# A hybrid gMLP / gated delta rule layer in three phases, with most of its large products formed by Strassen's method

## The chip, the cores and the metric

The kernel runs on one core of a Trainium2 chip. The metric is device time in microseconds of one execution. Engines are named as in the profile: PE (TensorE, the matrix engine), PEld (its weight loads), DVE (VectorE), ACT (ScalarE), POOL (GpSimd) and SP (SyncE, which here only issues DMAs). A matmul takes a stationary block (the weight load) and streams the columns of a moving block past it; "columns" below are those of the moving block.

## The reference

One layer takes 2048 prompt tokens and 8 single sample tokens through one combined projection, two branches and a merge. Cut to its core:

```python
h = rmsnorm(x, pre_g)
u_a, v_a, z_a, qkv, z_b, a_b, b_b, gate_a, gate_b = jnp.split(h @ w_in, splits, axis=-1)
y_a = u_a * (W_s @ rmsnorm(v_a) + b_s) * silu(z_a)          # 128-position chunks, tril W_s
q, k, v = silu(short_conv(qkv, width 4));  q, k = l2norm(q), l2norm(k)
# gated delta rule per head: S_t = a_t S_{t-1} + k_t beta_t (v_t - a_t S_{t-1}^T k_t)^T,  o_t = S_t^T q_t
y_b = rmsnorm(o, gdn_g) * silu(z_b)
merged = sigmoid(gate_a) * (y_a @ w_pa) + sigmoid(gate_b) * (y_b @ w_pb)
out = x + rmsnorm(merged @ w_out, post_g)
```

The model width is 1024, with 8 heads of 128. There are 12 kinds of large products, each 2056 tokens by 1024 by 1024: nine column groups of `w_in` (u, v, z, q, k, v of the conv, z_b, gate a, gate b), and `w_pa`, `w_pb`, `w_out`. All is fp32. The outputs are also the new conv rows, the matrix states and the normalised v rows.

## The kernel before

**Tiling.** The tokens are cut in two halves: f = 0 with 1024 tokens and f = 1 with 1024 tokens and the 8 samples. `TBS` cuts half 0 in 2 blocks of 512 columns and half 1 in 3 of 344. Every fp32 factor is held as the sum of a high and a low part in the type fp32r, and a product takes three matmuls for each of 8 blocks of 128 features: high by high, high by low, low by high.

**The stream of products.** A `Job` is one block of 128 output features. `load()` brings its 512 KB of weights, `split()` makes the parts (ACT the high one at L147, DVE the low one in two pieces at L149), `products()` puts 24 matmuls per token block on PE at L161, and the job's `evac` takes the result out of PSUM. `run()` goes through all jobs of half 0, of half 1 and of the end phase, loading and splitting one job ahead.

**What lies between the products.** `products()` counts streamed columns, and after every `STRIDE` = 2800 it calls `step()`, which advances one generator of each of four queues: chains (`chq`), small work (`smq`), convolutions (`cvq`) and heads (`bgq`). The order of instructions on every engine follows from these calls. `head()` does one head of one half: transposes of k and q, KD, E, M and AT, then a substitution of 31 dependent steps on DVE (L511 to L513: shuffle, multiply, subtract), spread over 28 yields, then the merge of its blocks to X and Y. `chain()` then goes through 8 chunks of 128 tokens, one after another: p (PE), r (DVE, L585), pz (PE), w (ACT, L591), pu (PE), S (DVE, L596), and S is what the next p needs. O is the output of a chunk.

**Where.** The sixteen heads (8 of each half) lie beside the products of `w_in`; the products of `w_pa`, `w_pb` and `w_out` come last, from about 2160 us, with no head beside them. The normalised x is built by `build_h()` (L245 and its split L203/L204). The beginning has its own order for the v products of half 0 (L933).

Of the kernel before, what the change touches and what calls it, by code (L numbers as in the profile page):

```python
# [25 lines left out]
PIN = True  # L26


def hybrid_step(tc, d):
    nc = tc.nc  # L30
    if PIN:
        mm = lambda *a, **k: tc.keep_in_program_order(nc.tensor.matmul(*a, **k))  # L32
        transpose = lambda *a, **k: tc.keep_in_program_order(nc.tensor.transpose(*a, **k))  # L33
    else:
        mm, transpose = nc.tensor.matmul, nc.tensor.transpose
    top = ExitStack()
    cp = top.enter_context(tc.tile_pool(name="cp", bufs=1))
    ap = top.enter_context(tc.tile_pool(name="apool", bufs=1))
    wp = top.enter_context(tc.tile_pool(name="wp", bufs=2))
    tp = top.enter_context(tc.tile_pool(name="tp", bufs=3))  # L40
    dp = top.enter_context(tc.tile_pool(name="dp", bufs=1, space=DRAM))
    pa = top.enter_context(tc.tile_pool(name="pa", bufs=3, space=PSUM))

    dma = nc.sync.dma_start

    def big():
        return tp.tile([P, 3, 344], F32, tag="big", name="big", bufs=4)

    flat = lambda t: t.rearrange("p a b -> p (a b)")

# [19 lines left out]
    S = cp.tile([P, NH, P], F32, name="S")  # L70
    nc.gpsimd.memset(S, 0.0)
# [3 lines left out]
    ssx = cp.tile([P, 17], F32, name="ssx")  # L75
    nc.gpsimd.memset(ssx[:, 16:17], 1.0)
# [3 lines left out]
    nwt = cp.tile([P, 64], F32, name="nwt")  # L80

# [1 line left out]
    m_sp = [[dp.tile([P, WT[f]], F32, name=f"m{f}_{g}") for g in range(8)] for f in range(2)]  # L83
    ya_sp = [dp.tile([8, P, WT[f]], F32, name=f"ya{f}") for f in range(2)]
# [39 lines left out]
    class Job:  # L124
        def __init__(self, w, acts, tbs, evac, pre=None, mid=None, m=P):
            self.w, self.acts, self.tbs, self.evac, self.pre, self.mid, self.m = w, acts, tbs, evac, pre, mid, m
            self.raw = self.hi = self.lo = self.ahead = None

        def last(self, b):
            return b == len(self.tbs) - 1  # L130

    def load(j):
        if j.raw is None:
            j.raw = wp.tile([P, KB, P], F32, tag="raw", name="raw", bufs=1)
            dma(j.raw[:, :, :j.m], j.w)

    def load_apart(j):
        j.raw = sp.tile([P, KB, P], F32, tag="KD", name="raw1", bufs=2)
        dma(j.raw, j.w)

    def split(j):
        if j.hi is None:
            load(j)
            j.hi = wp.tile([P, KB, P], F32R, tag="hi", name="hi")
            j.lo = wp.tile([P, KB, P], F32R, tag="lo", name="lo")
            m = j.m
            nc.scalar.activation(j.hi[:, :, :m], j.raw[:, :, :m], AF.Copy)  # L147
# [3 lines left out]
    streamed = [0]

    def products(j, b):
        off, w = j.tbs[b]
        ah, al = j.acts
        ps = pa.tile([P, 512], F32, tag="acc", name="acc")
        out = ps[:j.m, :w]
        i = 0
        for k in range(KB):
            for wt, at in ((j.hi, ah), (j.hi, al), (j.lo, ah)):  # L160
                nc.tensor.matmul(out, wt[:, k, :j.m], at[:, k, off:off + w], start=(i == 0), stop=(i == 23))  # L161
                i += 1
                streamed[0] += w
                if streamed[0] >= STRIDE:
                    streamed[0] -= STRIDE
                    step()
        j.evac(b, ps, off, w)
        if j.mid:
            j.mid(b)

    def run(groups):
        jobs = [j for g in groups for j in g]
        pos = 0
        for g in groups:
            for j in g:
                split(j)
                if j.pre:
                    j.pre()
            last = g[-1]
            nxt = jobs[pos + len(g): pos + len(g) + 2]  # L180
            for b in range(len(last.tbs)):
                if g[0].ahead:
                    g[0].ahead(b)
                for j in g:
                    if b == 0 and nxt:
                        load(nxt[0])
                    if len(g) == 1:
                        if b == 1 and nxt:
                            split(nxt[0])
                    elif j is last and j.last(b) and nxt:  # L190
                        split(nxt[0])
                    products(j, b)
            pos += len(g)

    def wblk(i):
        return d["w_blk"][i]

# [1 line left out]
    def new_set(pool, pre):  # L199
        return [pool.tile([P, KB, 1032], F32R, name=pre + n) for n in "hl"]  # L200
# [12 lines left out]
    def build_h(f, off, w, at, start=False):  # L213
# [27 lines left out]
        while got:  # L241
# [5 lines left out]
            if todo:  # L247
                got.append(fetch())
# [996 lines left out]
```

## Time and profile before

| | |
|---|---|
| runs | 2706.78 us median of 3 (2701.3 to 2707.1) |
| span of the profiled execution | 2705.5 us |
| PE matmul busy | 2615.8 us, 97% |
| PE weight load busy | 2334.3 us, 86% |
| DVE / ACT / POOL busy | 1553.0 / 1044.4 / 420.7 us |
| moved by DMA | 280 MB, 31% of the queues' time |
| chain that ended last | PE 78%, DVE 11%, DMA 5%, ACT 3% |

The profiled execution lies 1.3 us below the median of the runs. The busy time of a matmul is longer than the distance to the next one, since matmuls follow each other in a pipeline; so counts times start-to-start distances tell what PE needs, and busy time tells only where it stood still.

### The profile page before, as it was taken

The page shows a single profiled execution, that of the slowest core. Times are in us where ns is not written, and L with a number is a line of the kernel's source. Part 1 is how long each engine was busy: PE and PEld are TensorE (multiplying, and loading weights), DVE is VectorE, ACT ScalarE, POOL GpSimd, SP SyncE. Part 2 cuts the span into 40 slices and gives each one's busy share as a digit, 9 for nine tenths or more (in the row PEclk, how much of TensorE's full clock was granted, in tenths as well). Part 3 has the DMA queues.
Part 4 walks back from the last instruction along what each step waited for, and adds up shares of the span by engine and source line. Part 5 has one row for each costly group of instructions (what it writes and reads, how often), then busy time and mean ns, then how long its engine had stood idle before and what let it go on. Part 6 is the DMA issues. An engine that isn't in the chain of part 4 may idle for free.

```text
span 2705.5 us, 42484 instructions
## 1 busy us (share of the span) xinstructions
PE 2615.8 (97%) x15755; PEld 2334.3 (86%) x15755; DVE 1553.0 (57%) x5001; ACT 1044.4 (39%) x2728; POOL 420.7 (16%) x535
## 2 busy tenths in 40 slices
PE   7989999999999999989999999999998999999998
PEld 6778788887788888989999999999998988999886
DVE  6266866765765725356668657567565444442454
ACT  5323453453453423423534534534431332332121
POOL 2021111121121102022112211211202102102000
PEclk9989999999999999999999999999999999999999
DMA  6232212211211223123122122112145676645442
GB/s 205 79 121 63 67 43 71 86 44 59 79 44 67 86 77 115 48 70 108 56 65 68 48 76 72 42 68 75 46 133 202 221 245 233 243 168 183 136 141 95
DMA packets 139792, 280.38 MB, mean 104 GB/s; under 512 B 19944, under 2 KB 75688, under 8 KB 139584
## 3 DMA queue, kind: packets, MB, share of 16 engines
q1 hardware_dynamic: 139584, 277.66, 31.0%
q8 instruction: 124, 2.03, 0.3%
q14 instruction: 84, 0.69, 0.1%
HBM read 205.06 MB, written 72.55 MB: 103 GB/s over the span
## 4 chain that ended last, share of the span: by engine, by line
PE 78%; DVE 11%; DMA 5%; ACT 3%; issue 1%; POOL 1%; SPq 0%; DVEq 0%; ACTq 0%; POOLq 0%
PE acc L161 64%; PE p L32 2%; PE acc L933 2%; PE O L32 2%; DVE vT L653 2%; PE trn L33 2%; PE pu L32 1%; PE g L32 1%; DVE lo L149 1%; PE pz L32 1%; PE pk L32 1%; DMA m<-mo 1%; DVE bc L511 1%; DVE nwt L96 1%; DMA xt<-in_x_tok 1%
## 5 line engine op out<-in xcount | busy, mean ns | idle before, releaser
L161 PE MATMUL acc<-Ah,hi 128*128 128x344 f32 (+1 forms) x3360 | 1202.2, 358 | 1.4 <-ACT Ah L203 1.4
L161 PE MATMUL acc<-Ah,lo 128*128 128x344 f32 (+1 forms) x3360 | 1201.0, 357 | 0.3 <-DVE lo L149 0.3
L161 PE MATMUL acc<-Al,hi 128*128 128x344 f32 (+1 forms) x3360 | 1199.4, 357 | 0.5 <-DVE Al L204 0.2
L161 PEld LDWEIGHTS acc<-Al,hi 128*128 128x128 f32 x3360 | 636.1, 189 | 57.7 <-DVE Al L204 1.4
L161 PEld LDWEIGHTS acc<-Ah,lo 128*128 128x128 f32 x3360 | 636.6, 189 | 57.1 <-DVE lo L149 0.6
L161 PEld LDWEIGHTS acc<-Ah,hi 128*128 128x128 f32 x3360 | 636.2, 189 | 57.1 <-ACT Ah L203 1.9
L149 DVE TENSOR_TENSOR lo<-raw,hi 128x512 fp32r<-128x512 f32 x370 | 266.3, 739 | 313.4 <-ACT hi L147 278.8
L147 ACT ACTIVATE hi<-raw 128x1024 fp32r<-128x1024 f32 x185 | 195.3, 1056 | 320.6 <-PE acc L161 282.8
L513 DVE TENSOR_TENSOR Yc<-Yc,tmp 128x248 f32<-128x248 f32 (+30 forms) x496 | 148.6, 300 | 10.2
L511 DVE STREAM_SHUFFLE bc<-Uc 128x248 f32<-128x248 f32 (+30 forms) x496 | 151.1, 309 | 0.0
L512 DVE TENSOR_TENSOR tmp<-bc,Yc 128x248 f32<-128x248 f32 (+30 forms) x496 | 145.7, 294 | 0.5
L481 POOL TENSOR_TENSOR kl<-kq,kh 128x256 fp32r<-128x256 f32 x128 | 97.9, 773 | 238.1 <-ACT kh L480 237.9
L653 DVE SCALAR_TENSOR_TENSOR kq<-craw,convw,kq 128x1024 f32<-128x1024 f32 x96 | 122.6, 1277 | 1.1
L591 ACT ACTIVATE w<-pz,s_bb 128x128 f32<-128x128 f32 x128 | 46.9, 367 | 184.4 <-PE pz L32 184.1
L585 DVE SCALAR_TENSOR_TENSOR r<-p,neg,NV 128x128 f32<-128x128 f32 x128 | 44.2, 346 | 126.7 <-PE p L32 126.2
L161 PE MATMUL acc<-Bh,hi 128*128 128x344 f32 (+1 forms) x320 | 111.9, 350 | 0.0
L161 PE MATMUL acc<-Bh,lo 128*128 128x344 f32 (+1 forms) x320 | 111.9, 350 | 0.0
L161 PE MATMUL acc<-Bl,hi 128*128 128x344 f32 (+1 forms) x320 | 111.6, 349 | 0.0
L1101 POOL TENSOR_TENSOR g<-g,u 128x344 f32<-128x344 f32 (+1 forms) x40 | 45.1, 1128 | 349.1 <-DVE g L1100 344.9
L637 ACT ACTIVATE craw<-acc 128x344 f32<-128x344 f32 (+1 forms) x120 | 61.1, 509 | 94.1 <-PE acc L161 93.8
L446 ACT ACTIVATE junk<-trn 128x128 f32<-128x128 f32 x256 | 67.4, 283 | 42.3 <-PE trn L33 42.3
L1100 DVE TENSOR_TENSOR g<-g,acc 128x344 f32<-128x344 f32 (+1 forms) x40 | 23.2, 581 | 101.6 <-PE acc L161 83.5
(321 smaller groups left out, 3485.3 us busy)
## 6 DMA issues: line engine op xcount, KB each, us to landing
raw<-in_w_blk SPq DMA_DIRECT2D x136, 512.0 KB, 3.7
g<-big SPq DMA_DIRECT2D x16, 516.0 KB, 3.2
g<-g SPq DMA_DIRECT2D x16, 516.0 KB, 4.8
xt<-in_x_tok SPq DMA_DIRECT2D x16, 512.0 KB, 4.8
m<-mo SPq DMA_DIRECT2D x32, 256.0 KB, 3.1
G<-gc SPq DMA_DIRECT2D x16, 512.0 KB, 9.0
g<-big SPq DMA_DIRECT2D x16, 512.0 KB, 2.8
yb<-yT SPq DMA_DIRECT2D x32, 256.0 KB, 2.3
```

Source lines behind the costliest of these rows:

```text
L32: mm = lambda *a, **k: tc.keep_in_program_order(nc.tensor.matmul(*a, **k))
L33: transpose = lambda *a, **k: tc.keep_in_program_order(nc.tensor.transpose(*a, **k))
L147: nc.scalar.activation(j.hi[:, :, :m], j.raw[:, :, :m], AF.Copy)
L149: nc.vector.tensor_tensor(j.lo[:, p, :m], j.raw[:, p, :m], j.hi[:, p, :m].bitcast(F32), ALU.subtract)
L161: nc.tensor.matmul(out, wt[:, k, :j.m], at[:, k, off:off + w], start=(i == 0), stop=(i == 23))
L446: nc.scalar.activation(junk, tr[:, tk(n)], AF.Square, accum_out=acc[:, c:c + 1])
L481: nc.gpsimd.tensor_tensor(kl, kq[:, :, tk(c)], kh.bitcast(F32), ALU.subtract)
L511: nc.vector.stream_shuffle(bc[:, :, l + 1:], Uc[:, :, l + 1:], [l] * 32)
L512: nc.vector.tensor_tensor(tmp[:, :, l + 1:], bc[:, :, l + 1:], Yc[:, :, l:l + 1].to_broadcast([P, 8, 31 - l]), ALU.mult)
L513: nc.vector.tensor_tensor(Yc[:, :, l + 1:], Yc[:, :, l + 1:], tmp[:, :, l + 1:], ALU.subtract)
L637: nc.scalar.activation(raw[:, 3 + off:3 + off + w], ps[:, :w], AF.Copy)
L653: nc.vector.scalar_tensor_tensor(acc, raw[:, i:i + HALF], convw[:, blk, i:i + 1], acc, ALU.mult, ALU.add)
```

## The change

The kernel is cut in three phases, and the tokens of half 1 in two quarters of 516 columns (512 prompt tokens and 4 samples each; `NQ`), each streamed as 2 × 258.

**Phase 1** forms v, the three conv kinds, z, u of both halves, and z_b of half 0. Two blocks of 128 output features are taken as a `Pair`, and with the two quarters of tokens they form a 2 × 2 by 2 × 2 block product: `seven()` takes 7 products of 4 feature blocks each where the plain way takes 8. `weights()` forms the 7 weight operands of a pair, split in parts; `refill()` forms the 7 token operands of a half once, at the start and at the switch to half 1. k, q, v, z_b, m and y_a of all heads go to DRAM. **Phase 2** forms z_b of half 1, both gates and `w_pa` by plain products (L754), and all sixteen heads lie beside these; `fetch_unit()` brings a head's k, q, v back. A `step()` now comes every 1700 columns, and the substitution has 12 yields. **Phase 3** forms `w_pb` and `w_out` by `seven()`.

```diff
-TB3 = [(0, 344), (344, 344), (688, 336)]
-TBS = [[(0, 512), (512, 512)], [(0, 344), (344, 344), (688, 344)]]
-STRIDE = 2800
+NQ = [512, 516]
+TBS = [[(0, 512), (512, 512)], [(0, 258), (258, 258), (516, 258), (774, 258)]]
+PACE = [2800, 1700, 2800]
...
+    def parted(src, tag, k):
+        hi, lo = wtile(tag + "h", k=k), wtile(tag + "l", k=k)
+        nc.scalar.activation(hi, src, AF.Copy)
+        nc.vector.tensor_tensor(lo, src, hi.bitcast(F32), ALU.subtract)
...
+    def weights(p):
+        r1, r2 = wtile("r1", F32), wtile("r2", F32)
+        dma(r1, p.w1)
+        dma(r2, p.w2)
+        yield
+        a, b, c, e = r1[:, 0:4, :], r1[:, 4:8, :], r2[:, 0:4, :], r2[:, 4:8, :]
+        p.wt[0], p.wt[2] = parted(r1, "wa", 8)
+        nc.gpsimd.tensor_tensor(a, a, c, sub)
+        nc.vector.tensor_tensor(c, c, e, add)
+        yield
+        p.wt[5] = parted(e, "wx", 4)[0]
+        nc.vector.tensor_tensor(e, e, a, sub)
+        nc.gpsimd.tensor_tensor(b, b, e, sub)
+        yield
+        p.wt[4], p.wt[1] = parted(r2, "wc", 8)
+        yield
+        p.wt[3], p.wt[6] = parted(r1, "wb", 8)
...
+        for k in range(4):
+            for wp_, at in ((hi, ah), (hi, al), (lo, ah)):
+                for b in range(n // w):
+                    nc.tensor.matmul(ps[:m, b, :w], wp_[:, k, :m], at[:, k, b * w:(b + 1) * w], ...)
+                    stream(w)
...
+    def seven(p, ops, n, nxt, after):
+        A = acc()
+        go(0, A)
+        nc.scalar.activation(cv(s1[:, :n], n), pv(A, n), AF.Copy)
+        B = acc()
+        go(1, B)
+        nc.vector.tensor_tensor(cv(u2[:, :n], n), pv(B, n), cv(s1[:, :n], n), ALU.add)
+        go(2, A)
+        p.evac(0, 0, A, None, n)
+        go(3, B)
+        nc.vector.tensor_tensor(cv(u3[:, :n], n), pv(B, n), cv(s1[:, :n], n), ALU.add)
+        C = acc()
+        go(4, C)
+        p.evac(1, 1, C, u3, n)
+        go(5, B)
+        p.evac(1, 0, B, s1, n)
+        go(6, C)
+        p.evac(0, 1, C, u2, n)
...
-            if (l + 1) * 28 // 31 > l * 28 // 31:
+            if (l + 1) * 12 // 31 > l * 12 // 31:
                 yield
```

With `n` = 516 a product is 24 matmuls of 258 columns, with `n` = 512 it is 12 of 512 columns. The numbers of pairs are 28 (half 0) and 24 (half 1) in phase 1, and 4 of each width plus 8 of 512 columns in phase 3.

How the order stands on the engines, at three places. First DVE, where the convolutions of k and q of the first head lie. Before (`lo` is a weight's low part, L650 and L653 the convolution, `mo` the gMLP mix, `rx` a statistic of x):

```order
L149 TENSOR_TENSOR lo<-raw,hi 128x512
L650 TENSOR_SCALAR kq<-craw,convw 128x1024
L418 SCALAR_TENSOR_TENSOR mo<-mx,vecs,bb 128x512
L98 SCALAR_TENSOR_TENSOR rx<-nwt,rx 128x9
L653 SCALAR_TENSOR_TENSOR kq<-craw,convw,kq 128x1024
L418 SCALAR_TENSOR_TENSOR mo<-mx,vecs,bb 128x512
L653 SCALAR_TENSOR_TENSOR kq<-craw,convw,kq 128x1024
L149 TENSOR_TENSOR lo<-raw,hi 128x512
L653 SCALAR_TENSOR_TENSOR kq<-craw,convw,kq 128x1024
```

After, on DVE in one pair of a conv kind in phase 1 (`wal`, `wxl`, `wcl`, `wbl` are low parts of weights, `r` their sums, `u` and `q<-acc` sums out of PSUM, L559 the convolution):

```order
L217 TENSOR_TENSOR u_3033<-acc,s_3015 128x512
L559 SCALAR_TENSOR_TENSOR q<-q,convw 128x512 x6
L146 TENSOR_TENSOR wal<-r_2987,wah 128x1024
L225 TENSOR_TENSOR u_3068<-acc,s_3015 128x512
L158 TENSOR_TENSOR r_2988<-r_2988 128x512
L543 TENSOR_TENSOR q<-acc,u_3068 128x512
L543 TENSOR_TENSOR q<-acc,s_3015 128x512
L146 TENSOR_TENSOR wxl<-r_2988,wxh 128x512
L161 TENSOR_TENSOR r_2988<-r_2988,r_2987 128x512
L543 TENSOR_TENSOR q<-acc,u_3033 128x512
L146 TENSOR_TENSOR wcl<-r_2988,wch 128x1024
L146 TENSOR_TENSOR wbl<-r_2987,wbh 128x1024
```

Between the products of a pair DVE now has five sums out of PSUM and two of weights that it did not have, and low parts of seven operands rather than of two blocks.

Second DVE during a substitution with a chain beside it. Before, from one r to the next:

```order
L585 SCALAR_TENSOR_TENSOR r<-p_4750,neg,NV 128x128
L512 TENSOR_TENSOR tmp<-bc,Yc 128x8x29
L511 STREAM_SHUFFLE bc<-Uc 128x8x28
L513 TENSOR_TENSOR Yc<-Yc,tmp 128x8x29
L511 STREAM_SHUFFLE bc<-Uc 128x8x27
L512 TENSOR_TENSOR tmp<-bc,Yc 128x8x28
L596 SCALAR_TENSOR_TENSOR S<-S,s_eg,pu 128x128
L513 TENSOR_TENSOR Yc<-Yc,tmp 128x8x28
L511 STREAM_SHUFFLE bc<-Uc 128x8x26
L512 TENSOR_TENSOR tmp<-bc,Yc 128x8x27
L689 TENSOR_TENSOR big<-acc,big 128x512
L513 TENSOR_TENSOR Yc<-Yc,tmp 128x8x27
```

After, from one S to the next:

```order
L998 SCALAR_TENSOR_TENSOR S<-S,s_eg,pu 128x128
L912 TENSOR_TENSOR Yc<-Yc,tmp 128x8x29
L910 STREAM_SHUFFLE bc<-Uc 128x8x27
L911 TENSOR_TENSOR tmp<-bc,Yc 128x8x28
L987 SCALAR_TENSOR_TENSOR r<-p_13816,neg_80,NV 128x128
L912 TENSOR_TENSOR Yc<-Yc,tmp 128x8x28
L910 STREAM_SHUFFLE bc<-Uc 128x8x26
L911 TENSOR_TENSOR tmp<-bc,Yc 128x8x27
L912 TENSOR_TENSOR Yc<-Yc,tmp 128x8x27
L910 STREAM_SHUFFLE bc<-Uc 128x8x25
L911 TENSOR_TENSOR tmp<-bc,Yc 128x8x26
L998 SCALAR_TENSOR_TENSOR S<-S,s_eg,pu 128x128
```

The number of iterations from one chunk to the next is about the same, three to five, though fewer columns of products now lie on PE between the two.

Third PE inside a chunk of the chain, with `acc` the products. Before, in half 0, and ending with the next p:

```order
L32 MATMUL pz<-r,Y 128x128
L32 MATMUL O<-S,kq 128x128
L161 MATMUL acc<-Ah,lo 128x512
L161 MATMUL acc<-Ah,hi 128x512
L161 MATMUL acc<-Al,hi 128x512
L161 MATMUL acc<-Ah,lo 128x512
L161 MATMUL acc<-Ah,hi 128x512
L161 MATMUL acc<-Al,hi 128x512
L32 MATMUL pu<-w,KD 128x128
L32 MATMUL O<-w,AT 128x128
```

After, beside the products of half 1:

```order
L31 MATMUL pz<-r,Y 128x128
L31 MATMUL O<-S,kq 128x128
L754 MATMUL acc<-yh,hi 128x258
L754 MATMUL acc<-yl,hi 128x258
L754 MATMUL acc<-yh,lo 128x258
L31 MATMUL pu<-w,KD 128x128
L31 MATMUL O<-w,AT 128x128
```

Between pz and pu, where ACT makes w, six matmuls of 512 columns stood; now three to five of 258 do.

## Rows read from the trace of the kernel before

**Rows 1.** Page, busy time, share of the span and instructions of each engine.

```profile
PE 2615.8 (97%) x15755; PEld 2334.3 (86%) x15755; DVE 1553.0 (57%) x5001; ACT 1044.4 (39%) x2728; POOL 420.7 (16%) x535
```

**Rows 2.** Groups by form, PE (count | busy us, mean ns | idle before).

```profile
L161 PE MATMUL acc<-Ah,hi 128*128 128x344 f32 x1952 | 637.2, 326 | 1.4 <-ACT Ah L203 1.4
...
L161 PE MATMUL acc<-Ah,hi 128*128 128x512 f32 x1376 | 553.5, 402 | 0.0
...
L933 PE MATMUL acc<-wvhi,Ah 128*128 128x512 f32 x64 | 27.3, 426 | 4.6 <-ACT Ah L203 4.6
```

**Rows 3.** Timeline of a chunk of the chain (start, duration, what).

```profile
1005.91 0.40 PE L161 MATMUL acc<-Al,hi 128*128 128x512 f32 x1
...
1006.14 0.40 PE L161 MATMUL acc<-Ah,lo 128*128 128x512 f32 x1
...
1006.84 0.38 PE L32 MATMUL pz<-r,Y 128*128 128x128 f32 x2
...
1007.06 0.39 PE L32 MATMUL O<-S,kq 128*128 128x128 f32 x2
...
1007.32 0.37 ACT L591 ACTIVATE w<-pz,s_bb 128x128 f32<-128x128 f32 x1 [4.74 <-PE pz L32]
...
1008.45 0.38 PE L32 MATMUL pu<-w,KD 128*128 128x128 f32 x2
...
1008.87 0.35 DVE L596 SCALAR_TENSOR_TENSOR S<-S,s_eg,pu 128x128 f32<-128x128 f32 x1 [2.88 <-PE pu L32]
```

**Rows 4.** Timeline of PE around a wait in half 1.

```profile
1352.85 0.35 PE L32 MATMUL pk<-kh 128*128 128x256 f32 x1 [1.83 <-DVE nwt L97]
...
1353.16 0.28 PE L32 MATMUL pk<-kh,kl 128*128 128x256 f32 x1
1353.28 0.32 PE L161 MATMUL acc<-Ah,lo 128*128 128x344 f32 x1
1353.44 0.32 PE L161 MATMUL acc<-Ah,hi 128*128 128x344 f32 x1
...
1354.26 0.49 PE L161 MATMUL acc<-Ah,lo 128*128 128x344 f32 x1
```

**Rows 5.** Windows (stretch, length, busy of PE PEld DVE ACT POOL, PEclk, DMA).

```profile
0.00:60.00 60.00, 45.13 (x179) 34.61 (x180) 38.87 (x142) 33.91 (x91) 15.73 (x32) 0.97 0.66 222
...
340.00:1080.00 740.00, 725.26 (x4160) 600.43 (x4159) 457.61 (x1555) 315.46 (x838) 126.09 (x154) 1.00 0.21 70
...
1240.00:2000.00 760.00, 739.39 (x5362) 722.46 (x5361) 514.68 (x1890) 343.88 (x960) 132.89 (x197) 0.99 0.21 66
```

**Rows 6.** Groups by form, DVE.

```profile
L149 DVE TENSOR_TENSOR lo<-raw,hi 128x512 fp32r<-128x512 f32 x368 | 266.0, 742 | 309.2 <-ACT hi L147 274.6 <-PE acc L161 33.4 <-PE pz L32 1.0
...
L585 DVE SCALAR_TENSOR_TENSOR r<-p,neg,NV 128x128 f32<-128x128 f32 x128 | 44.2, 346 | 126.7 <-PE p L32 126.2
...
L1153 DVE TENSOR_TENSOR ob<-acc,postg 128x512 f32<-128x512 f32 x32 | 22.0, 688 | 10.8 <-ACT jk L1152 10.5
...
L97 DVE SCALAR_TENSOR_TENSOR nwt<-nwt,tot 128x1 f32<-128x1 f32 x48 | 7.6, 159 | 1.7
```

**Rows 7.** Page, the costliest groups: the three instructions of the substitution.

```profile
L513 DVE TENSOR_TENSOR Yc<-Yc,tmp 128x248 f32<-128x248 f32 (+30 forms) x496 | 148.6, 300 | 10.2
L511 DVE STREAM_SHUFFLE bc<-Uc 128x248 f32<-128x248 f32 (+30 forms) x496 | 151.1, 309 | 0.0
L512 DVE TENSOR_TENSOR tmp<-bc,Yc 128x248 f32<-128x248 f32 (+30 forms) x496 | 145.7, 294 | 0.5
```

**Rows 8.** Timeline, DVE and POOL reading side by side.

```profile
1058.08 1.11 POOL L204 TENSOR_TENSOR Al<-big,Ah 128x344 fp32r<-128x344 f32 x1 [0.98 <-ACT Ah L203]
1058.32 1.24 DVE L245 SCALAR_TENSOR_TENSOR big<-big,vecs,prs 128x344 f32<-128x344 f32 x1
```

**Rows 9.** All instructions of line L245 (durations in ns: least, median, most).

```profile
L245 DVE SCALAR_TENSOR_TENSOR big<-big,vecs,prs x24: 564/574/1294, 1052.3 to 1076.5; 128x344 f32<-128x344 f32 x24
```

**Rows 10.** Timeline of the opening: PE's first product.

```profile
12.36 0.80 PE L933 MATMUL acc<-wvhi,Ah 128*128 128x512 f32 x1 [3.48 <-ACT Ah L203]
```

More of the change, by code (lines that the diff above doesn't have):

```diff
@@ L151, in hybrid_step @@
[L151 to L193, printed above, removed]
@@ new lines, in none, with run_pairs @@
+    def none(s):
+        pass
+    def run_pairs(pairs, sets):
+        for i, (p, s) in enumerate(pairs):
+            ops, n, filler = sets[s]
+            last = i + 1 == len(pairs) or pairs[i + 1][1] != s
+            nxt = pairs[i + 1][0] if i + 1 < len(pairs) else None
+            gen = filler() if last and filler else None
+            run_all(p.prep) if i == 0 else None
+            seven(p, ops, n, nxt, (lambda s_: next(gen, None)) if gen else none)
+            if gen:
+                run_all(gen)
@@ new lines, in ab_products @@
+    def ab_products(f, ops):
+        n = NQ[f]
+        w = n if n <= 512 else n // 2
+        ab = p1.tile([32, WT[1]], F32, tag="ab", name="ab")
+        for tq in range(2):
+            ps = acc()
+            terms = ((0, 0), (1, 2)) if tq == 0 else ((0, 4), (0, 0), (1, 6))
+            for b in range(n // w):
+                for i, (kh, s) in enumerate(terms):
+                    for k in range(4):
+                        for j in range(2):
+                            nc.tensor.matmul(ps[0:32, b, :w], abw[:, kh * 4 + k, :], ops[s][j][:, k, b * w:(b + 1) * w],
+                                             start=i + k + j == 0, stop=i == len(terms) - 1 and k == 3 and j == 1)
+                            stream(w)
+            nc.scalar.activation(cv(ab[:, tq * n:(tq + 1) * n], n), pv(ps, n, 32), AF.Copy)
+        return ab
@@ new lines, in run @@
+    def run(groups):
+        for gi, g in enumerate(groups):
+            nxt = groups[gi + 1] if gi + 1 < len(groups) else []
+            for j in g:
+                split(j)
+                if j.pre:
+                    j.pre(j)
+            nb = len(TBS[g[0].f])
+            for b in range(nb):
+                for j in g:
+                    if b == 0:
+                        for x in nxt:
+                            load(x)
+                    if b == nb // 2 and j is g[0] and nxt:
+                        split(nxt[0])
+                    if b == nb - 1 and j is g[-1] and len(nxt) > 1 and len(g) == 1:
+                        split(nxt[1])
+                    products(j, b)
@@ new lines, in hybrid_step @@
+    groups2 = []
+    for i, js in enumerate(sets2):
+        if i < 3:
+            js[-1].mid = turn(i)
+        groups2 += [js[0:2]] + [[j] for j in js[2:-2]] + [js[-2:]]
+    A[0][1] = (ytile("h"), ytile("l"))
+    split(groups2[0][0])
+    split(groups2[0][1])
+    h_quarter(1, 0, 1, pr_rows(1, 1))
+    fetch_unit(0)
+    for f, h in units:
+        bgq.append(head(f, h))
+    smq.append(samples())
+    run(groups2)
+    drain()
+    main.close()
+    late = ExitStack()
+    pace[0] = PACE[2]
```

1201 lines of the change are left out of this document (653 added, 548 removed).

## The prediction

> **What bounds the kernel now.** The page comes first: PE is busy 97% of the span, its weight loads 86%, DVE 57% and POOL 16% [rows 1]. A matmul's busy time overlaps the next one's, so the distances of starts count. In half 0 the products start 0.23 us apart at 512 columns [rows 3], in half 1 0.16 us at 344 [rows 4]. Per column that is 0.451 ns in both, so I count 0.231 and 0.156 us. There are 4944 products of 512 columns (3 × 1376 and 6 × 64 have their forms in [rows 2], `w_pb` of half 0 adds 384, the samples of `w_out` 48) and 6480 of 344 or 336 (3 × 1952 [rows 2], 576 of `w_pb` in half 1, and 48). That makes 1142 + 1011 = 2153 us. All other matmuls, counted likewise (5 × 256 of p, pz, pu and two O at 0.11, the rows of transposes and small blocks), need 359 us. PE needs 2512 of 2705.5 us, and 193 us are lost: to waits, to small gaps and to stretches at half clock. The windows show where waits lie: 15 us of the first 60, 15 of 340 to 1080 and 21 of 1240 to 2000 [rows 5]; the last two hold about 7 heads each, so a head leaves PE idle for only 2.5 us. PE's supply of columns bounds the kernel, and the delta rule hides beside the products, with DVE busy 62 to 68% there [rows 5]. A wait costs more than itself: after one of 1.83 us the matmuls of 344 columns go on for a few us at 0.49 us duration instead of 0.32, the granted clock being then at its lower level, 1.2 GHz rather than 2.4 [rows 4].
>
> **The change part by part.**
>
> *Products.* A pair takes 7 products of 12 matmuls of 512 columns (84), or 168 of 258. After, 512 columns: 28 × 84 in phase 1, 48 × 24 in phase 2, 12 × 84 and 48 for the samples in phase 3, together 4560 × 0.231 = 1053 us. 258 columns: 24 × 168, 32 × 96 and 4 × 168, together 7776. No row has 258 columns. At 0.451 ns a column one is 0.1175 us with its fixed part; the nearest row is pk, 256 columns with another block each time, 0.12 us from one to the next (1353.16 to 1353.28 in [rows 4]). The upper bound is the 0.156 of 344 columns, if a weight load sets the distance. I take 0.1175, since pk is two columns away: 914 us. Sum 1967, **186 less** than 2153.
>
> *Other PE work.* The heads' matmuls stay. New are 64 more transposes of v (7 us), the statistics of x on PE (10) and the pieces cut in quarters (some 12): **29 more**. PE's need becomes 2512 − 186 + 29 = 2355 us: phase 1 1092, phase 2 940 (627 of products, 313 of heads), phase 3 323.
>
> *Loss in phase 1.* A conv pair of 512 columns is 19.4 us on PE. Beside it DVE has five sums out of PSUM at 0.69 (the nearest row is L1153 [rows 6]), 12 convolution steps of 512 at about the same (8.3), low parts of 3 × 1024 and 512 weights (seven times the 0.74 row less overlap, 4.5 [rows 6]) and two weight sums (1.2): 16 to 18 us. It fits, with little left. ACT has 566 and POOL 333 us in the phase, which fit. I charge 28 us of steady loss for 52 pairs (0.55 each). The opening before has its first product at 12.36 us [rows 10] and loses 15 in 60; now four tiles of 1 MB, their norm, and the first of seven operands stand ahead of it, and later operands interrupt the first pair: 30 us, bounds 15 (as before) and 55 (all 7 operands in a row on DVE). The switch to half 1 makes 7 operands beside one pair: 10. Closing the phase: 5. **Loss 73.**
>
> *Loss in phase 2.* Sixteen heads lay beside about 155,000 columns of products each; now beside 80,000, 36 us. PE has 940/16 = 58.8 us per head. DVE's work in a head is the same: substitution (151 + 146 + 149)/16 = 27.8 us [rows 7], 8 each of r, S, M, KD, E, AT at about 0.34 = 16 [rows 6], low parts 5, two inverse roots 5, yT, transposes and gate sums 9: 63 us by durations, 54 to 59 by distances of starts, since its instructions overlap a little. So DVE, at 60% before, nearly equals PE. In the substitution DVE has three to five iterations per chunk as before but 23 products of 258 columns (2.7 us) rather than 17 of 512 (3.9) beside them; its 27.8 us, r and S of five chunks (3.4) and two low parts (1.5), less a little overlap, make about 32 us of DVE where the order puts 28.5 us of PE work: 3.5 lost per head. The hand-over from pz to pu took 0.95 us before the earliest pu: 0.48 until w began, 0.37 for w, and about 0.1 more [rows 3]. pz and O need 0.44 of it; three products of 258 fill 0.35, five fill 0.59: 0.16 lost at worst, 1 us a head. From pu to S and p (0.42 + 0.35 + 0.1) six and more products stand, which covers it. The merge has one more wait, 1.5; half clock after waits 1.5, and small gaps 1.5. Together 9 us a head, bounds 2.5 (as before [rows 5]) and 16 (below). 16 × 9 = 144, and 15 at the opening of the phase, when the first head stands without a chain and PE waits for a fetched k. **Loss 159.**
>
> POOL's work grows from 421 to about 760 us. Beside a POOL instruction that reads, a DVE instruction of two inputs took 1.24 us [rows 8], where its median is 0.574 [rows 9].
>
> The Trainium skill (SBUF — State Buffer, Who interferes with whom) says that a DVE instruction with two SBUF inputs and a GpSimd instruction that reads SBUF exclude each other for a whole instruction; this trace agrees, with 1.24 against 0.574 us. By it the 340 us of added POOL work could lengthen DVE by up to that much; the 3.5 us per head above hold none of it.
>
> *DMA.* Spilled and fetched again are k, q, v of the conv, v and z_b, some 42 MB each way beside 280; the queues are busy 0.21 of the time in the stages of the heads [rows 5], so I cost this at nothing. If a fetch came late, the head that waits for it would pay the few us of one landing.
>
> *Loss in phase 3.* Opening (`w_pb`'s tokens staged after the last head, and its operands): 25 us, bounds 12 and 40. In a pair of `w_out` DVE has some 17 us against PE's 19.4: six PSUM sums and products at 0.69 (4.1), low parts 4.5, weight sums 1.2, four 512 wide closing steps 3, and 22 small steps of two inverse roots, each waiting for the one before, 3.5 to 4 [rows 6]. These stand in the queue ahead of the sums that free PSUM for the next product; I charge 1.5 us a pair, 12 for eight. Two refills 12, the samples and the tail 13. **Loss 62.**
>
> *Sum.* 2355 + 73 + 159 + 62 = 2649. In terms of before: 186 saved, 29 more, losses 294 instead of 193: 2705.5 − 186 + 29 + 101 = 2650. The profiled span is 1.3 us below the median of the runs, so it is the time forecast as well: **2650 us**, 2.1% less.
>
> **The rivals.**
>
> *Losses stay in proportion.* The new order keeps PE as full as before, with 193/2705 = 7.1% lost. For it: chains still have a product behind each wait, and only 2.5 us a head were lost. Against it: DVE nearly equal to PE in phase 2, two more openings. 2355/0.929 = 2535 us.
>
> *DVE's serial path sets phase 2, and the kernel is slower.* In a head the steps from M to Xc, then Y's merge, and the chain of the head before must pass DVE one after another, and the next head's merge waits until the chain is done. If DVE meets POOL and ACT at every hand-over, the substitution takes 37 us instead of 32, the rest of DVE's work 21, and hand-overs that nothing covers 17: 75 us a head, 16 × 75 + 15 = 1215; with phases 1 and 3 as above (1165 and 385) 2765 us. It decides from 71.3 us a head, where the sum is 2706. For it: 63 us of DVE durations per head, and single steps at twice their length beside POOL [rows 8]. Against it: before, with the same DVE work per head, r waited for p for 126 of its 127 us of idle time [rows 6], so DVE was the one that waited, and the chain of one head runs beside the substitution of the next.
>
> *The weight load sets the distance at 258 columns.* Each load is busy 2334.3/15755 = 0.148 us in the mean [rows 1], more than 0.1175. At 0.156 the 7776 products cost 300 us more: 2950 us. For it: loads are 86% busy. Against it: 344 columns at 0.156 go with loads that overlap, and pk changes its block every 0.12 us [rows 4].
>
> The Trainium skill (Perfetto Trace Analysis, Identifying the Most-Contended Engine) holds that headroom is judged by MFU (the share of the matrix engine's peak) and the weight loads' busy share, not by matmul busy time. By that rule a change that lifts product loads from 11424 to 12336 would not shorten a kernel with loads at 86%; pk's 0.12 us speaks against it here.
>
> **How the numbers follow.** The forecast has a chance of 0.56 (2570 to 2715, by its bounds: phase 1 from 1140 to 1195, phase 2 from 1060 to 1140, phase 3 from 370 to 400), losses in proportion 0.21, DVE's path 0.18 (2706 to 2830), the weight load 0.05. The range 2520 to 2760 leaves out half of the DVE case, the weight load and a few parts of the others. About 0.2% (5 us) is what a measurement of this kernel can tell from no change. Faster by more: the forecast below 2701 and the losses in proportion, 0.73. Within: 0.05. Slower: 0.22.
>
> **What would show it right or wrong.** Products of 258 columns 0.117 us apart, and PE's windows in phase 1 at 1165 us, phase 2 at 1100, phase 3 at 385 confirm the sum. In phase 2 PE should wait for DVE's S and r above all, and DVE be above 80% busy. Wrong would be: distances near 0.156 us (the load), phase 2 below 1020 us (the losses stay), or 71 us and more a head with DVE waited for at the substitution's end (DVE's path), or a phase 1 in which PE waits for DVE's sums out of PSUM at most pairs.

## The result, and the profile of the changed kernel

The changed kernel takes 2997.3 us (median of 4 runs) against 2705.0 us: 1.108 times as long, 95% interval 1.106 to 1.111. The forecast was 2650 us, 2% faster; the time lies far outside the range, on the other side. First the page of the changed kernel: the engines, then PE and its granted clock in 40 slices.

```profile
PE 2619.1 (87%) x16923; PEld 2283.2 (76%) x16923; DVE 2082.7 (69%) x5452; ACT 1226.3 (41%) x2988; POOL 913.8 (30%) x852
...
PE   6899799998898999989999998999889794768798
...
PEclk9899899999999999998999999999999887889899
```

Beside [rows 1], PE is busy 87% of the span instead of 97%, and the clock line has nine slices under 9 where the page before had one. The stretches of the three phases and of the gap between the last two (length, busy of PE, PEld, DVE, ACT, POOL, PEclk, DMA) answer to [rows 5]:

```profile
0.00:100.00 100.00, 56.26 (x205) 46.33 (x206) 48.84 (x76) 29.19 (x34) 27.85 (x14) 0.85 0.28 99
100.00:1341.00 1241.00, 1133.79 (x6905) 997.97 (x6903) 808.07 (x1053) 457.46 (x856) 413.27 (x428) 0.97 0.33 108
1341.00:2499.00 1158.00, 1064.73 (x8087) 945.34 (x8087) 867.34 (x3794) 586.90 (x1869) 238.72 (x285) 0.96 0.39 126
2499.00:2535.00 36.00, 0.00 (x0) 0.00 (x0) 21.38 (x31) 8.96 (x12) 8.67 (x3) 0.57 0.90 327
2535.00:2997.00 462.00, 364.33 (x1728) 293.58 (x1728) 337.05 (x500) 143.81 (x220) 225.33 (x122) 0.90 0.44 140
```

As in the prediction, PE's need is the count of matmuls times their distances, and the loss is the rest; the 128 matmuls of the statistics of x, 28 us, stand under the loss. Need is an estimate: with the median distance for every small matmul, that of phase 2 comes to 949 us rather than 933. The loss splits into waits (PE idle for more than 0.6 us), what the lower clock costs at most (half of PE's busy time at 1.2 GHz), and the rest:

| | need, forecast | need | loss, forecast | loss | of it waits | lower clock, at most | rest |
|---|---|---|---|---|---|---|---|
| phase 1, to 1341 us | 1092 | 1087 | 73 | 248 | 127 | 40 | 81 |
| phase 2, to 2499 us | 940 | 933 | 159 | 224 | 90 | 40 | 94 |
| gap and phase 3 | 323 | 323 | 62 | 167 | 121 | 29 | 17 |
| sum | 2355 | 2343 | 294 | 639 | 338 | 109 | 192 |

The first 7 and last 9 us come on top and make the span. Before, counted in the same way, need was 2512 and loss 177 (waits 68, lower clock at most 29), with 16 us at the ends. So the saving in need came as forecast, 169 us, and the loss grew by 462, of which 270 are waits. First, a piece of PE's timeline in phase 1, half 1:

```profile
1000.15 0.40 PE L191 MATMUL acc<-yl,wch 128*128 128x258 f32 x2
1000.39 0.40 PE L191 MATMUL acc<-yh,wcl 128*128 128x258 f32 x2
```

Two matmuls of 258 columns take 0.24 us, so one takes 0.12, like pk in [rows 4], and the weight load does not bind. What PE waited for (total us, times, longest):

```profile
PE acc L191 <- DVE u L225: 72.2, 46, 5.8
PE acc L191 <- ACT wah L145: 43.3, 4, 36.2
PE otr L32 <- ACT OS L1010: 38.0, 27, 2.7
PE acc L191 <- DVE wal L146: 23.0, 4, 10.0
```

`u L225` is the sum u3 of a pair: PE may not add the next product, `go(5, B)`, to accumulator B before DVE has read B. The 36.2 us at `wah` is the gap before phase 3. How u3 comes late is seen in a timeline of one conv pair (start, duration; in brackets the idle time before and what ended it):

```profile
517.45 1.06 ACT L145 ACTIVATE wah<-r 128x1024 fp32r<-128x1024 f32 x1 [6.00 <-DMA r<-in_w_blk]
...
518.48 0.40 PE L191 MATMUL acc<-th,wbl 128*128 128x512 f32 x1
...
518.54 1.23 DVE L146 TENSOR_TENSOR wal<-r,wah 128x1024 fp32r<-128x1024 f32 x1 [4.43 <-ACT wah L145]
...
519.83 0.75 DVE L559 SCALAR_TENSOR_TENSOR q<-q,convw 128x512 f32<-128x512 f32 x1
...
519.90 1.83 POOL L157 TENSOR_TENSOR r<-r,r 128x512 f32<-128x512 f32 x1 [7.05 <-DVE wal L146]
...
521.77 0.69 DVE L158 TENSOR_TENSOR r<-r 128x512 f32<-128x512 f32 x1 [1.18 <-POOL r L157]
...
522.38 0.75 DVE L559 SCALAR_TENSOR_TENSOR q<-q,convw 128x512 f32<-128x512 f32 x1
...
523.04 0.68 DVE L225 TENSOR_TENSOR u<-acc,s 128x512 f32<-128x512 f32 x1
...
523.78 0.50 PE L191 MATMUL acc<-th,wxh 128*128 128x512 f32 x1 [2.12 <-DVE u L225]
```

DVE first stands idle 4.43 us for wah, since `wal` is at the head of its queue; POOL's difference waits for `wal`, DVE's sum L158 waits for POOL, and u3 is behind all of them. The last matmul into its accumulator ends at 518.88 us and u3 begins at 523.04; in between DVE still stands idle for 1.18 us at L158, and when PE comes to wait, from 521.66 us on, DVE is busy with what it had put off.

### The profile page after: what moved, and what is told of

Same layout as the page of the kernel before. It is cut to its first block, busy times and chain, and to the rows that moved or that the text cites. A ratio compares the mean times of both kernels' runs of the same rounds, so it can differ in the third digit from the quotient of the medians.

```text
span 2996.9 us, 47123 instructions
## 1 busy us (share of the span) xinstructions
PE 2619.1 (87%) x16923; PEld 2283.2 (76%) x16923; DVE 2082.7 (69%) x5452; ACT 1226.3 (41%) x2988; POOL 913.8 (30%) x852
## 5 line engine op out<-in xcount | busy, mean ns | idle before, releaser
L754 PE MATMUL acc<-yh,hi 128*128 128x258 f32 (+1 forms) x1408 | 462.2, 328 | 12.9 <-ACT hi L739 10.1
L754 PE MATMUL acc<-yl,hi 128*128 128x258 f32 (+1 forms) x1408 | 462.2, 328 | 0.9 <-DVE yl L244 0.6
L754 PE MATMUL acc<-yh,lo 128*128 128x258 f32 (+1 forms) x1408 | 462.0, 328 | 0.0
L754 PEld LDWEIGHTS acc<-yh,hi 128*128 128x128 f32 x1408 | 274.4, 195 | 26.6 <-ACT hi L739 10.2
L754 PEld LDWEIGHTS acc<-yl,hi 128*128 128x128 f32 x1408 | 274.7, 195 | 14.8 <-POOL yl L244 1.1
L754 PEld LDWEIGHTS acc<-yh,lo 128*128 128x128 f32 x1408 | 274.2, 195 | 12.3 <-DVE lo L741 0.2
L191 PE MATMUL acc<-yh,wah 128*128 128x258 f32 (+2 forms) x784 | 230.8, 341 | 59.9 <-ACT wah L145 43.3
L559 DVE SCALAR_TENSOR_TENSOR q<-q,convw 128x512 f32<-128x512 f32 x288 | 234.9, 838 | 37.6 <-ACT q L557 34.6
L191 PE MATMUL acc<-yh,wal 128*128 128x258 f32 (+2 forms) x784 | 231.3, 342 | 23.0 <-DVE wal L146 23.0
L191 PE MATMUL acc<-yl,wah 128*128 128x258 f32 (+2 forms) x784 | 230.8, 340 | 3.8 <-DVE yl L244 3.8
L191 PEld LDWEIGHTS acc<-yh,wah 128*128 128x128 f32 (+1 forms) x784 | 135.8, 193 | 80.2 <-ACT wah L145 44.4
L191 PE MATMUL acc<-th,wxh 128*128 128x258 f32 (+1 forms) x384 | 121.7, 365 | 72.2 <-DVE u L225 72.2
L191 PEld LDWEIGHTS acc<-yh,wal 128*128 128x128 f32 (+1 forms) x784 | 135.9, 194 | 41.4 <-DVE wal L146 24.7
L191 PEld LDWEIGHTS acc<-yl,wah 128*128 128x128 f32 (+1 forms) x784 | 136.1, 193 | 21.3 <-DVE yl L244 4.6
L191 PE MATMUL acc<-th,wch 128*128 128x258 f32 (+1 forms) x384 | 112.9, 342 | 37.6 <-ACT th L243 19.4
```

The costliest lines, as they stand in the source:

```text
L191: nc.tensor.matmul(ps[:m, b, :w], wp_[:, k, :m], at[:, k, b * w:(b + 1) * w], start=first and i == 0, stop=i == 11, skip_group_check=True)
L559: nc.vector.scalar_tensor_tensor(o, raw[:, i:i + 512], convw[:, blk, i:i + 1], o, ALU.mult, ALU.add)
L754: nc.tensor.matmul(out, wt[:, k, :], at[:, k % 4, o:o + w], start=(i == 0), stop=(i == 23))
```

## Experiments

The times are of one execution of each kernel; the kernel before took 2705 to 2709 us beside them. Differences are to the changed kernel's 2997 us.

### Plain products in the same phases

In place of `seven()`, with the same pairs, staging and pools, four blocks of two products each:

```diff
+        for tq in range(2):
+            for i in range(2):
+                A = acc()
+                product(p.wt[2 * i], ops[4 * tq], A, n, True, False)
+                product(p.wt[2 * i + 1], ops[4 * tq + 2], A, n, False, True)
+                p.evac(i, tq, A, None, n)
...
```

The sums in `weights()` and `refill()` go too, four operands are split rather than seven, and the split weights have two buffers.

> Phases 1 and 3 with the same pairs, pools, staging and order, but eight plain products a pair: no sums of weights, of tokens or of products. PE's need grows by 145 us in phase 1 (to 1232) and 44 in phase 3 (to 367). Theory S (Strassen's sums are what costs): the loss of phase 1 falls from 236 to about 110 us and phase 3's from 131 to 60; phase 1 ends at about 1340 us as with seven products, phase 3 takes 430 rather than 497, the whole 2930 to 2960. Rival T (the three phases cost, with their openings and switches): the losses stay, phase 1 ends at 1470 us, phase 3 takes 500 to 530, the whole about 3170.

Measured: 2878.0 us, 119 less, although PE has 186 us more to do. Its stretches, phase 1 and phase 3:

```profile
0.00:1316.00 1316.00, 1286.75 (x7997) 1155.93 (x7998) 459.92 (x636) 451.40 (x863) 200.55 (x332) 1.00 0.34 109
...
2493.00:2876.00 383.00, 373.86 (x1968) 314.54 (x1968) 171.87 (x374) 93.00 (x152) 48.56 (x34) 0.99 0.55 172
```

The loss of phase 1 falls from 248 to 80 us (some 38 us of this in the first 100) and that of phase 3 without its gap from 131 to 7. S holds, more strongly than expected: by the seven-product form PE saves 186 us and loses 292. What of the 292 is due to the sums, and what to the fewer split operands and the second buffers, this run does not separate. T falls for these phases. But the phases themselves are not free either: 2878 is still 6% above the kernel before.

### Which part of the form: order, landing, DVE's load

Three links of the chain shown above are taken away one at a time. The first moves the emission of the weight work behind u3:

```diff
-        ahead()
         go(3, B)
         u3 = etile("u3")
         nc.vector.tensor_tensor(cv(u3[:, :n], n), pv(B, n), cv(s1[:, :n], n), ALU.add)
+        ahead()
```

> In each pair the weight work for the next pair (low part wal, POOL's difference, DVE's sum L158) is emitted behind the sum u3 instead of ahead of it; nothing else changes. Theory Q (queue): DVE's L158 waits for POOL, u3 stands behind it in DVE's queue, and PE waits for u3 before its sixth product; then the 72 us in which PE waits for u3, and the half clock behind them, fall to below 20 us, and the kernel takes 60 to 110 us less (about 2900). Rival W (work): DVE simply has too much to do in a pair; then the wait goes to another of the pair's sums and the time stays within 20 us of 2997.

Measured: 2987.0 us, 10 less, the waits for u3 71 us. It tells nothing on Q: the order on DVE is made by a scheduler, and in the timeline `wal` and L158 still stand ahead of u3. So the order was held in a second kernel, by pinning u2, u3, the low parts and DVE's two sums (with the same move):

```diff
+    vtt = lambda *a, **k: tc.keep_in_program_order(nc.vector.tensor_tensor(*a, **k))
...
```

> Here u2, u3 and the weight work on DVE are held in one order, so that u3 really stands ahead of wal and L158 in DVE's queue (in the first of these tries the scheduler had put them back). Theory Q (queue: wal waits for ACT, which waits until PE's third product has let go of the old operand, L158 waits for POOL, and u3 stands behind both): PE's waits for u3, 72 us, fall below 20; phase 1 and phase 3 together take 60 to 110 us less. Rival M (the chain of weight work is itself too long for a pair): the wait turns up at the next pair's wah, wal or wcl, and the time changes by less than 25 us.

Measured: 3000.6 us, no gain, phase 1 3 us shorter and phase 3 14 longer. M holds for the time. But the wait does not move to wah, wal or wcl, as M had it: PE's waits for u2 and u3 in phase 1 from 100 us on (both are L33 here) are 62.6 us, where they were 49.9. Now u3 stands ahead of `wal`, and is late all the same:

```profile
513.78 1.06 ACT L146 ACTIVATE wah<-r 128x1024 fp32r<-128x1024 f32 x1 [6.24 <-DMA r<-in_w_blk]
...
514.75 0.58 ACT L542 ACTIVATE q<-acc 128x512 f32<-128x512 f32 x1
...
515.41 0.72 ACT L558 ACTIVATE q<-q,convw 128x512 f32<-128x512 f32 x1
...
516.17 2.33 DVE L560 SCALAR_TENSOR_TENSOR q<-q,convw 128x512 f32<-128x512 f32 x3 [5.96 <-ACT q L558]
...
518.41 0.69 DVE L33 TENSOR_TENSOR u<-acc,s 128x512 f32<-128x512 f32 x1
```

```profile
PE acc L192 <- DVE u L33: 62.6, 39, 16.0
```

ACT's queue does to the convolution what DVE's did to u3: its copy L558 is behind wah, wah waits for the weights, and DVE's convolution steps, ahead of u3, wait for the copy. Next the load itself, by a second buffer for r1, paid with one of six buffers of q and with single buffers for three small tiles:

```diff
-        return ph["p"].tile([P, k, P], dt, tag=tag, name=tag, bufs=1)
+        return ph["p"].tile([P, k, P], dt, tag=tag, name=tag, bufs=2 if tag == "r1" else 1)
...
```

> The raw weights r1 of a pair get two buffers rather than one (in phases 1 and 3; paid with one q buffer of six and single buffers of small mix tiles), the order of instructions stays nearly the same. Theory L (landing): r1's load can start only when the pair before has read r1 for the last time; ACT's wah waits for it, DVE's wal for wah at the head of its queue (111 us idle in phase 1), u3 stands behind wal, PE behind u3. Then PE's 72 us of waits for u3 fall below 25 and phases 1 and 3 take 60 to 120 us less. Rival W (DVE has too much to do in a pair): wal is early, but u3 stays late; less than 25 us.

Measured: 2991.5 us, 6 less, with phase 1 itself 7 longer and PE's waits for u3 still 72 us; L falls. What ACT's wah waited for in phase 1 tells why, the changed kernel first, then this one:

```profile
ACT wah L145 <- DMA r<-in_w_blk: 117.8, 28, 7.3
```

```profile
ACT wah L145 <- PE acc L191: 119.1, 32, 6.2
```

The weights are there, and the same 119 us are now waited for PE, which still reads the one buffer of the split operand until its third product ends. A second buffer for that, with the seven products kept, was not tried. Last the amount of DVE's work:

```diff
-            nc.vector.scalar_tensor_tensor(o, raw[:, i:i + 512], convw[:, blk, i:i + 1], o, ALU.mult, ALU.add)
+            if i == 3:
+                nc.vector.scalar_tensor_tensor(o, raw[:, i:i + 512], convw[:, blk, i:i + 1], o, ALU.mult, ALU.add)
```

> Leaves out two of the three DVE steps of every convolution (192 of 288 instructions of 0.84 us, 160 us of DVE work in phase 1). Rival W (DVE has too much to do in a pair): the waits for u3 in phase 1 fall from 42 us to below 12 and the phase takes 60 us less or better. Theory L (u3 stands behind a wait for the weights' landing): DVE only waits longer at wal, and phase 1 changes by less than 25 us.

Measured: 2953.0 us. Phase 1 is 37 us shorter and PE's waits for u3 in it fall from 42.5 to 27.3 us: between the two expectations. DVE's load is a part of it, a fifth of phase 1's excess over the forecast, not the cause.

### Which part of the form: weight sums, product sums

The two kinds of sums were then left out one at a time: in one kernel the four sums of raw weights, in the other s1, u2 and u3 with the additions in `evac`.

```diff
-        nc.gpsimd.tensor_tensor(a, a, c, sub)
-        nc.vector.tensor_tensor(c, c, e, add)
...
-        nc.vector.tensor_tensor(e, e, a, sub)
-        nc.gpsimd.tensor_tensor(b, b, e, sub)
```

> Leaves out the four sums of raw weights in every pair (two on POOL, two on DVE), and so the steps in which DVE, POOL and ACT wait for each other's sums; seven products, splits, loads and the sums of products stay. Theory V (the chain of weight sums through three engines holds the pair up): PE's 72 us of waits for u3 fall below 25, phases 1 and 3 together take 100 us less or better. Theory U (the sums out of PSUM between dependent products hold it up): less than 40 us.

```diff
...
-        nc.vector.tensor_tensor(cv(u2[:, :n], n), pv(B, n), cv(s1[:, :n], n), ALU.add)
...
-        nc.vector.tensor_tensor(cv(u3[:, :n], n), pv(B, n), cv(s1[:, :n], n), ALU.add)
...
-        p.evac(1, 1, C, u3, n)
+        p.evac(1, 1, C, None, n)
...
```

> Leaves out the sums out of PSUM: s1, u2 and u3 are not formed, and the four blocks of a result leave PSUM as the plain products do (three of them on ACT rather than DVE); weight sums and all products stay. So PE's products of one accumulator follow without DVE between them. Theory U: the loss of phases 1 and 3, 248 + 131 us, falls by 150 us or more, near the 87 of eight plain products. Theory V: PE now waits for the split weights (wah, wal, wcl) instead, and the gain is below 60 us.

Measured: 2851.6 us without weight sums, 146 less; 2862.7 us without product sums, 135 less. In the first, phase 1 takes 92 us and phase 3 48 us less; in the second 78 and 52. V was expected to give 100 or more and gives 140; U to give 150 and gives 130. So neither kind of sum alone makes up the 292 us that plain products give back, and the two gains cannot be added up. Some 95 of the 292 us lie where the seven operands of the tokens are formed, a third kind of sums, and stay for the most part: 38 in the first 100 us, and at the switch of halves and two refills of phase 3 PE's waits of over 1 us are 60 us in the changed kernel, 52 without weight sums, 63 without product sums and at most 4 with plain products. The other 197 us are less than the two gains together (270, some 250 of it outside these places), so by this estimate a part of them goes away with either kind: it needs both. A kernel with seven products and neither kind was not run. Leaving out the weight sums also takes work from POOL and DVE, so their gain is that of the chain and of the work together. PE's wait for u3 itself hangs on the weight sums. In the kernel without them DVE still waits 111 us for wah in all (129 in the changed kernel), but nothing that PE needs is held back long by it; this is what is left of PE's waits for u3 in its phase 1 from 100 us on, and below it the same for the changed kernel:

```profile
PE acc L187 <- DVE u L221: 4.1, 1, 4.1
```

```profile
PE acc L191 <- DVE u L225: 42.5, 35, 4.1
```

### The opening

All of the statistics' work is left out: the squares on ACT, the matmuls and the sums. The edit is cut to the matmuls.

```diff
...
-                for b in range(4):
-                    for k in range(4):
-                        mm(ps[:, b:b + 1], s[:, k, b * P:(b + 1) * P], uinc[:, P - 1:P], start=k == 0, stop=k == 3)
...
```

> Leaves out the statistics of x of half 0 (ACT's squares, 128 matmuls of one column, the sums), so that the norm's factors are constants. Theory O (the 128 matmuls of one column, 0.217 us each, and the squares ahead of them are what makes the opening long): PE's first product begins at 14 to 17 us rather than 29, phase 1 ends 25 to 40 us earlier. Rival R (the operands' sums and splits on DVE, ACT and POOL set the opening): less than 12 us.

Measured: 2963.4 us, 34 less; phase 1 ends 31 us earlier and the first product begins at 19.2 us rather than 29.3. O holds in size, though the start came later than expected. The products reach the distances of the higher clock at 26 us rather than 60. The row of the changed kernel for one of the two groups of 64:

```profile
6.98 13.91 PE L31 MATMUL pst<-cst,sqx 128*128 128x1 f32 x64 [6.98 <-ACT sqx L349]
```

### Phase 2

```diff
+            if l % 3 == 0:
                 bc = sp.tile([P, 8, 32], F32, tag="bc", name="bc", bufs=2)
```

> Leaves out two of three iterations of each substitution on DVE, with all yields and everything else in place: some 18 us of DVE work per head, 290 us in phase 2, are taken away. Rival D (DVE is short in phase 2): phase 2's loss of 271 us falls by half or more, to below 140, and the kernel takes 120 us less or better. Theory P (hand-overs with too few columns behind them, then half clock): the waits for OS, w and the merge stay, and the time falls by less than 50 us.

The condition holds for the three instructions of an iteration. Measured: 2969.1 us, 28 less; phase 2 to its last product takes 1122 us rather than 1158, with DVE's busy time there down from 867 to 672 us. D falls: DVE's work in the substitution is not what phase 2 mainly waits for. (The waits for OS do fall, from 38 to 23 us, while those for r rise from 10.5 to 19.)

```diff
-PACE = [2800, 1700, 2800]
+PACE = [2800, 3400, 2800]
...
+                for rep in range(2):
+                    nc.tensor.matmul(out, wt[:, k, :], at[:, k % 4, o:o + w], start=(i == 0), stop=(i == 47))
...
```

> In phase 2 every product matmul is issued twice (the sums come out doubled) and a step comes every 3400 columns, so that each hand-over of the delta rule has twice the columns beside it and PE needs 627 us more. Theory P (each hand-over has too few columns behind it): the loss of phase 2, 271 us with its end, falls to about 100, and the kernel takes 450 to 480 us more, about 3460. Rival B (the loss lies in phase borders, merges and the small matmuls of the heads, whatever the columns): 580 to 630 us more, about 3600.

Measured: 3528.5 us, 531 more for 627 us of added need. The loss of phase 2 with the gap falls from 260 to 157 us, waits from 127 to 79 and the cost of the lower clock from at most 40 to 17. The result lies between the two: about 100 us of the loss are too few columns beside the hand-overs; 157 do not go away with columns.

```diff
-            for _ in range(6):
+            for _ in range(10):
                 yield
             tr = pg.tile([P, 512], F32, tag="tr", name="otr")
```

> In a chain, ten yields rather than six lie between OS and its transposes (in phase 2 only). Theory P (pace): what was six steps of 2800 columns is now six of 1700, so the way through ACT, eleven small DVE steps and ACT again is no longer covered; with ten steps the 38 us in which PE waits for OS fall to below 8, with the half clock behind them, 40 to 60 us less in phase 2, less up to 15 for the longer chain. Rival D (DVE is short in phase 2): the wait only moves to the chain's S and r, and the time stays within 15 us.

Measured: 3088.8 us, 91 more. PE's waits for OS beside the products fall from 38 to 12 us, as P says, and those for r rise from 10.5 to 39, as D says. But what decides is a third thing that neither named, in these two stretches, to the last product and after it:

```profile
1351.00:2414.00 1063.00, 987.53 (x7521) 884.10 (x7522) 785.44 (x3388) 539.29 (x1710) 211.01 (x263) 0.97 0.37 122
2414.00:2623.00 209.00, 108.48 (x569) 90.23 (x567) 111.39 (x439) 52.77 (x168) 31.22 (x25) 0.54 0.41 133
```

The products are used up 85 us earlier, and what is left of the heads then runs alone for 209 us, with PE busy for half of it at a mean granted clock of 0.54. On this reading phase 2 has columns for sixteen heads at the pace of 1700 and for no more: a hand-over can get more cover only by taking it from another.

```diff
+            for _ in range(6):
+                mm(tr[:, 0:P], ident, ident, start=True, stop=True)
```

> Ahead of the four transposes of OS in every half of a chain, six matmuls of the identity with itself into the same PSUM tile, 12 x 0.108 = 1.3 us of PE work that needs nothing, 32 times, 42 us in all. Theory C (the wait for OS costs twice, itself and then a stretch at half clock): PE no longer stands still there, the half clock behind these waits is gone, and the kernel takes 10 to 40 us less in spite of the added work. Rival N (the half clock is not set off by these waits): 10 to 40 us more.

Measured: 3026.8 us, 30 more. The waits for OS fall to 18.6 us and those for r rise to 24.7; PE is at the lower clock for 98 us of phase 2, against 88. The time is as N expected, but the test is weaker than it was meant to be: the added matmuls themselves (`otr L31`) wait at the same place, so that PE still stands still there for 29 of the 38 us.

```profile
PE otr L32 <- ACT OS L1010: 18.6, 16, 3.4
PE otr L31 <- DVE nwt L91: 5.1, 3, 2.1
PE otr L31 <- DVE rko L92: 3.1, 2, 2.0
PE otr L31 <- DVE nwt L90: 2.1, 1, 2.1
```

What sets off the lower clock in phase 2 is open; filling the other waits was not tried.

## Why the prediction was wrong

**Products and PE's need: right.** 258 columns take 0.12 us, and need fell by 169 us without the statistics (the forecast of 157 held 10 for them, so 167). The rival of the weight load falls.

The Trainium skill (Perfetto Trace Analysis, Identifying the Most-Contended Engine) would judge headroom by MFU and the weight loads' busy share. Here the share fell from 86% to 76% while the time rose by 11%, so it shows headroom that opened where PE stood still, and in that the trace agrees with the page. What the prediction drew from it, that more loads at 86% could not go faster, the trace does not bear out: a load is busy for 0.19 us (the median at L191 and L754), and products of 258 columns, each with its own load, follow every 0.12 us.

**Phase 1: the step "It fits, with little left" failed.** It weighed DVE's 16 to 18 us of work per pair against PE's 19.4 and charged 0.55 us a pair. DVE was indeed busy for only 808 of 1241 us. But inside one pair u3 stands behind a path through DMA or PE, ACT, DVE, POOL and DVE, and in the timeline above DVE stood idle at an instruction of this path while u3 was ready. The prediction named the sums and their durations, and did not follow what is queued ahead of them. Beside the opening and the switch of halves about 140 of the 248 us are lost, 2.7 us a pair. How much of this is u3's path is shown in part: PE's own waits for u3 from 100 us on are 42.5 us; leaving out the weight sums, and with them the path, gives back 92 us of the phase, the sums out of PSUM 78, two thirds of the convolution 37. The prediction's own sign, that PE waits for DVE's sums out of PSUM at most pairs, came true: 35 waits for u3 and 7 for u2 in 52 pairs. Before, PE waited for no evacuation of PSUM to speak of, as each block had its own accumulator; in this form DVE has to read B twice between products into it. The opening was the second mis-sized term: 80 us lost of the first 100, not 30. In these 80 are the statistics, charged as 10 us of need: they were 28 us of PE time, and 31 us of the phase. PE also ran at the lower clock until 60 us, where before that ended at 16 us; the prediction had no term for this. The switch of halves lost 28 us rather than 10.

**Phase 2: 224 us, not 159; 14 a head, inside the bounds of 2.5 and 16.** The waits came to 5.6 us a head, near the 6 that were charged, but not where they were charged: PE's transposes wait for OS, 38 us, a hand-over that was not priced, since a fixed six steps of the order are 10,200 columns at the new pace where they were 16,800; S and r, where PE was to wait above all, held it for 8.4 and 10.5 us. The mis-sized terms are half clock and small gaps, 1.5 us a head each: at most 2.5 and some 5.9 came. Of the small gaps 2.4 a head are the first product behind a small matmul, which at the higher clock takes 0.09 us more in the mean, 437 times; in these lines 0.21 us until the next start, and then 0.12:

```profile
1623.95 1.11 PE L32 MATMUL otr<-cst,OS 128*128 128x128 f32 x4 [1.45 <-ACT OS L1010]
1624.81 0.36 PE L754 MATMUL acc<-yh,hi 128*128 128x258 f32 x1
1625.02 0.28 PE L754 MATMUL acc<-yl,hi 128*128 128x258 f32 x1
1625.14 0.28 PE L754 MATMUL acc<-yh,lo 128*128 128x258 f32 x1
```

The kernel before had this too, 444 times and 39 us between 340 and 2000 us. The prediction's 2.5 us a head before was PE's idle time alone; counted by distances of starts, as its 193 us are, the same two stretches lost 84 us, 6 a head. So a head loses 8 us more than before, not 11. Beside it lie 86,000 columns where 180,000 lay; the prediction's 80,000 and 155,000 are both too low, and no term uses them. DVE was busy for 75% of the phase, not above 80. The rival of DVE's path was to decide from 71.3 us a head; phase 2 took 72.4, and 74.6 with the gap, but not by that mechanism: a substitution with a third of its iterations gave back 28 us (36 in the phase).

**Phase 3: 167 us, not 62.** Its opening lost 36 us with no matmul at all, a DMA share of 0.90 and then 12 us in the first pair, against 25 charged. The two refills of token operands, charged with 12, cost 39 us of waits. Of the lines below, 19.0 us of the first, all of the second and 11.5 of the third lie around them, at 2653 to 2675 and 2780 to 2802 us:

```profile
PE acc L191 <- DVE wal L146: 19.5, 3, 10.0
PE acc L191 <- ACT s L212: 8.3, 2, 4.2
PE acc L191 <- DVE u L225: 29.8, 11, 5.8
```

With the opening of the kernel and the switch, where the same seven operands are formed, that is 147 us against 52 charged (28 of the 147 are the statistics). Of the other 80 us of phase 3 leaving out one kind of sum gives back 48 or 52, and plain products lose only 7 us outside the gap. That they are the chain of phase 1 again is likely, and not shown.

**POOL and DVE.** DVE's weight sum L161 takes 0.69 us where POOL is still; this is its mean in phase 1 (1006 ns):

```profile
L161 DVE TENSOR_TENSOR r<-r,r 128x512 f32<-128x512 f32 x51 | 51.3, 1006 | 1.6
```

The Trainium skill (SBUF — State Buffer, Who interferes with whom) has two-input DVE instructions and reading GpSimd instructions exclude each other; the trace agrees, at 1.006 against 0.69 us. For this one line that is some 16 us over 51 pairs. Other lines of DVE are longer too: the convolution's L559 is 0.84 us in the mean of 288 and 0.75 in the timeline above, some 25 us more. What of this stands on PE's path was not measured.

## What to carry to other kernels

A method that trades matmuls for additions is to be priced by the path of one unit (here a pair) through all queues, from the release of its buffers to the matmul that needs its last sum, not by the busy time of each engine in it: DVE was busy 65% of phase 1 and still late. Saved columns are also lost cover, wherever dependent work hides beside them. And where a scheduler orders an engine, an edit that moves a statement may move no instruction: look at the order before measuring.

## What the runs showed of the hardware

A fp32 matmul of one column took 0.217 us (13.91 us for 64), as long as a fp32r matmul of 258 columns at the same level of the clock: a narrow matmul is not cheap. The lower level it ran at is read from its neighbours, as the profile has no granted clock before 60 us: products of 512 columns stand 0.43 us apart there, against 0.23 later. The 258 columns are from 1399.98 us, where the granted clock is 0.50. What one column takes at the higher level no run shows.

```profile
48.05 0.63 PE L191 MATMUL acc<-yh,wal 128*128 128x512 f32 x1
...
48.48 0.63 PE L191 MATMUL acc<-yh,wah 128*128 128x512 f32 x1
...
1399.98 0.42 PE L754 MATMUL acc<-yh,hi 128*128 128x258 f32 x1
1400.19 0.42 PE L754 MATMUL acc<-yl,hi 128*128 128x258 f32 x1
```

With 42 us of matmuls added at one place of phase 2, and 9 us less of standing still there, the time at the lower clock did not fall (98 and 88 us).
